# A two-layer hybrid block on one core: three feature groups by sevens in three gate-and-up blocks of each feed-forward layer, with other buffers for the weight loads

## The chip, the cores and the metric

The kernel runs on one core of one Trainium2 chip. The metric is the time of one execution on the device in microseconds (us). The kernel before takes 2230.15 us, the median of 3 runs (2229.86 to 2231.21).

The engines are named as in the profile. PE is TensorE, the matrix engine; PEld is its loading of the stationary operand, which runs beside the matmuls. DVE is VectorE, ACT is ScalarE, POOL is GpSimd, and SP is SyncE, which here only issues DMAs. All five run their own instruction streams in order and wait for each other at semaphores.

## What is computed

The input is 256 tokens of 2048 features in float32. There are two layers. The first has a gated delta rule beside a gated linear recurrence, the second two kinds of attention. Each is followed by a feed-forward part, which is the part that the change touches:

```python
def rmsnorm(x, w):
    xf = x.astype(jnp.float32)
    y = xf * lax.rsqrt(jnp.mean(xf * xf, axis=-1, keepdims=True) + NORM_EPS)
    return (y * w.astype(jnp.float32)).astype(x.dtype)

def swiglu(hn, w_gate, w_up, w_down):
    return (jax.nn.silu(hn @ w_gate) * (hn @ w_up)) @ w_down

def reference(x, ...):
    h = x
    for layer in range(DEPTH):
        ...
        h = h + swiglu(rmsnorm(h, ffn_norm[layer]), ffn_w_gate[layer], ffn_w_up[layer], ffn_w_down[layer])
    return rmsnorm(h, final_norm)
```

The gate and the up matrix are 2048 by 5632 each, the down matrix is 5632 by 2048, all float32 and read from HBM once.

## The kernel before

**Products in three matmuls.** A float32 weight tile of 128 by 1024 arrives by DMA (512 KB). ACT copies it into a type of fewer bits (`whi` or `thi`, line 608), DVE subtracts that from the original and keeps the rest (`wlo` or `tlo`, line 620). The activations `X` are kept as such a pair too. `Mix.add` then adds high by high (line 473), high by low (line 474) and low by high (line 475). So a weight tile costs an ACT cast, a DVE subtraction and some matmuls of 512 columns, and the second matmul of a tile is the first to need the low half.

**The feed-forward part** (`ffn`, line 720) works in three stages. A stage has four (the last one three) blocks of gate and up columns, 512 of each, and then two down blocks, which add the stage's inner values `hid` into the residual `h`. Within a block the contraction runs over feature groups of 512 features, of which a gate-and-up block has four. A group is done in one of two ways.

- *Plain* (`simple`): four weight tiles, each multiplied with both halves of the tokens, 12 matmuls a tile, 48 in all.
- *By sevens* (`seven`, line 490): a 2 by 2 block product with seven products in place of eight, 6 matmuls each, 42 in all. It needs sums of weight tiles and of activation tiles. Four tiles are loaded by SP: `ha` (called b11 in the code), `hb` (b12), `hc` (b22) and one that uses the tag `raw` (b21). DVE adds b12 into b11 (`first_sum`, line 503) and later b22 into it (`second_sum`, line 508). POOL issues two DMAs of 512 KB that add from HBM into a tile that is there already: b22 into b12 (line 504) and, later, b21 into b11 (line 512). The sums of activation tiles (`comb`) are made once per group by `combine_x` (line 404), on DVE with one cast on ACT, or by `combine` from a block's inner values.

A table (line 790) says how many groups of each block go by sevens. `(0, 2, 2, 2), (2, 2)` is the first stage: four gate-and-up blocks with none, two, two and two groups, then two down blocks with two each. I count the blocks of a layer from 0: 0 to 3 and 4, 5 are the first stage; 6 to 9 and 10, 11 the second; 12 to 14 and 15, 16 the third.

**Order.** `ffn` lists all steps of a layer in one order (lines 810 to 823), a step being one weight tile or sum and its matmuls. A block's steps by sevens are split: the first four products of every group (`early`) go between the last four plain steps of the block ahead (`tail`), the other three (`direct`) are mixed two to one with the block's own remaining plain steps (`body`). From block 1 on DVE, ACT and PE run just in the order in which `stream` (line 566) emits, with high halves made four steps ahead of the matmuls and low halves three. There are six buffers for high halves and five for low halves, so the low half of a step can be written only when PE has done the step five before it.

Other work hangs on this order by `puts`: when a block is done, `gate` and `product` make its inner values, `first` (line 729) transposes them on PE into `Ph` and copies them by ACT, `second` (line 746) makes their low half on DVE, and for the first blocks of a stage `combine` follows in parts on DVE (lines 396 and 401).

**Load buffers.** A step's tag names its buffers. `raw` has five, three of them in the pool `wr`, which is there for the whole kernel, and two in the phase's own pool `mx`; `ha`, `hb` and `hc` have two each in `mx`. Memory of a phase pool was used by the phase before, so its first user waits until that phase is over. In the first block of a layer, which is all plain, the tags `raw`, `ha`, `raw`, `hb`, `raw`, `hc` are taken in turn (line 487), to start with many buffers. `loads_to` (line 577) issues loads up to eight steps ahead, in the order of the steps. A tile's buffer comes free when the low half that is last to read it is done; for b11 that is the seventh product's.

Of the kernel before, what the change touches and what calls it, by code (L numbers as in the profile page):

```python
# [4 lines left out]
F32, F32R, I32 = dt.float32, dt.float32r, dt.int32  # L5
# [42 lines left out]
def body(tc, A, out):  # L48
    nc = tc.nc
# [7 lines left out]
    wr = pool("wr", 3)  # L57
# [4 lines left out]
    mx, ogp, fp = Phase(), Phase(), Phase()  # L62
# [18 lines left out]
    h = res.tile([128, 2, D], F32, name="h")  # L81
    X = res.tile([128, NK, 2, T], F32R, name="X", tag="X")
# [321 lines left out]
    def combine_x(x4, r=None):  # L404

        f = mx.tile([128, 4, T], F32, name="cf", **(dict(tag="de", bufs=1) if more else dict(tag="T", bufs=2)))
        V.tensor_tensor(out=f, in0=x4[:, :, 0].bitcast(F32), in1=x4[:, :, 1].bitcast(F32), op=ALU.add)
        return run(combine([f[:, :, t * 128:(t + 1) * 128] for t in range(2)], r))
# [36 lines left out]
    class Mix:  # L445
# [34 lines left out]
        def simple(self, i, u, first):  # L480
            b = {}

            def use(w, tt=(0, 1)):
                for t in tt:
                    self.add(t, i, lambda kk: self.xs(2 * u + kk, t), w)
            k = 2 * u + i
            return Step(("raw", "ha", "raw", "hb", "raw", "hc")[k % 6] if first and k < 10 else "raw",
                        lambda raw: nc.sync.dma_start(raw, self.src(i, u)), use, unit=(i, use))

        def seven(self, m):  # L490
# [75 lines left out]
    def stream(order, puts, guard):  # L566

        at = [0, 0, 0]
        where = {id(y): k for k, y in enumerate(order)}
        g = None

        slots, count_raw = {}, [0]

        def loads_to(n, must=False):
            while at[2] < min(n, len(order)):
                y = order[at[2]]
                if y.tag:  # L580
                    q = slots.setdefault(y.tag, [])
                    if len(q) == (5 if y.tag == "raw" else 2):
                        k = where[id(q[0])]
                        if k >= at[1]:
                            if not must:
                                return
                            low(k)
                        q.pop(0)
                    q.append(y.free)
                    if y.tag == "raw":  # L590
                        count_raw[0] += 1
                    y.raw = (wr.tile([128, 1024], F32, name="raw") if y.tag == "raw" and count_raw[0] % 5 in (0, 2, 4) else
                             mx.tile([128, 1024], F32, name=y.tag, tag=y.tag, bufs=2))
                    y.load(y.raw)
                at[2] += 1

        def ahead(n):

            while at[0] < min(n + 1, len(order)):
                y, k = order[at[0]], at[0]  # L600
                loads_to(k + 1, True)
                for z in y.needs:
                    low(where[id(z)])
                if y.ready:
                    y.raw = y.ready()
                y.hi = (fp.tile([128, 1024], F32R, name="thi", tag="thi", bufs=2) if k % 6 in (1, 4) else
                        wh.tile([128, 1024], F32R, name="whi"))
                S.copy(y.hi, y.raw)  # L608
                at[0] += 1
                if at[0] > 1:  # L610
                    low(at[0] - 2)
            while at[1] < min(n, len(order)):
                low(at[1])

        def low(k):
            while at[1] <= k:
                y, j = order[at[1]], at[1]
                y.lo = (fp.tile([128, 1024], F32R, name="tlo", tag="tlo", bufs=2) if j % 5 in (1, 3) else
                        wl.tile([128, 1024], F32R, name="wlo"))
                V.tensor_sub(y.lo, y.raw, y.hi.bitcast(F32))  # L620
                at[1] += 1
                if y.after:
                    y.after()

        for n, y in enumerate(order):
            for f in puts.get(n, []):
                f()
            if y is guard:
                g = tc.manual_schedule(engines={V.engine, S.engine, PE.engine})
                g.__enter__()  # L630
            loads_to(n + 8)
            ahead(n + 1 + 3)
            y.use((y.hi, y.lo))
            if y.unit:
                tick()
        for n in sorted(k for k in puts if k >= len(order)):
            for f in puts[n]:
                f()
        if g is not None:
            g.__exit__(None, None, None)  # L640
# [79 lines left out]
    def ffn(L, then, fin=None):  # L720

        gu, dn = A[f"gu{L}"], A[f"dn{L}"]
        cx, ch, blocks = {}, {}, []
# [64 lines left out]

        hid = ogp.tile([128, 16, 2, T], F32R, name="hid", tag="hid")
        b, events = 0, []  # L790
        for groups, down in (((0, 2, 2, 2), (2, 2)), ((2, 2, 2, 2), (2, 2)), ((2, 2, 2), (1, 1))):
            piece = len(groups)
            for j in range(piece + 2):
                space = (msp, "ms") if len(blocks) % 2 else (acc, "acc")
                if j < piece:
                    Y = Mix(lambda i, u, b=b: gu[b, u, i], lambda k: X[:, k], {m: lambda m=m: cx[m] for m in range(groups[j])}, 4,
                            *space, first=b == 0)
                    Y.after = values(Y, hid, j, j < max(down))
                    b += 1
                else:  # L800
                    p = j - piece
                    Y = Mix(lambda i, u, u0=2 * (b - piece), p=p: dn[2 * p + i, u0 + u], lambda k: hid[:, k],
                            {m: lambda m=m: ch[m] for m in range(down[p])}, piece, *space)
                    Y.after = residual(Y, p)
                blocks.append(Y)
# [5 lines left out]
        for Y in blocks:  # L811
            e = list(Y.early)
            r = -(-len(e) // len(tail)) if tail else 0
            while e or tail:
                order += e[:r] + tail[:1]
                e, tail = e[r:], tail[1:]
            cut = len(Y.plain) - 4 * (Y is not blocks[-1])
            d, body, tail = list(Y.direct), Y.plain[:cut], Y.plain[cut:]
            Y.first = (d + body + tail)[0]
            while d or body:  # L820
                order += d[:2] + body[:1]
                d, body = d[2:], body[1:]
            events += (Y.middle() if Y.ns else []) + Y.after
        where = {id(y): k for k, y in enumerate(order)}
# [4 lines left out]
        p0 = [where[id(y)] for y in blocks[0].plain]  # L829
        put(p0[5], lambda: cx.update({0: combine_x(X[:, 0:4])}))  # L830
        put(p0[8], rstd)
        put(p0[10], lambda: cx.update({1: combine_x(X[:, 4:8])}))
        Z, Y = blocks[-2:]
        q = where[id(Y.first)]
        if fin:
# [767 lines left out]
```

## Time and profile before

| | us |
|---|---|
| median of 3 runs | 2230.15 |
| the profiled execution, its time | 2229.7 |
| the profiled execution, its span from first to last instruction | 2227.5 |
| first layer's mixer, feed-forward part | 0 to 432, 432 to 1110 |
| second layer's mixer, feed-forward part and end | 1110 to 1524, 1524 to 2227 |

The limits of the stages are read from the chain of work that ended last. The page of the profile gives each engine's busy time, a strip of 40 slices, the DMA queues, that chain, and the costliest groups of instructions. In a row of instructions, `L620 DVE TENSOR_TENSOR wlo<-ha,whi` is line 620 on DVE, which writes `wlo` from `ha` and `whi`; in the timeline the first two columns are start and duration in us, `xN` merges N instructions in a row, and brackets at the end hold the idle time before it and who ended it. The duration of a pipelined instruction reaches beyond the start of the next one, so the distance of starts is what one costs in a full queue. In a list of waits the three numbers are the us in total, how often, and the longest.

### The profile page before, as it was taken

The numbers are of one execution on the slowest core, as the hardware profiler recorded it, in microseconds if no ns is written. First come the engines' busy times: TensorE is split into PE (matmuls) and PEld (weight loads), VectorE is DVE, ScalarE is ACT, GpSimd is POOL, SyncE is SP. The second block draws the span as 40 slices with busy tenths as digits, with TensorE's granted clock in tenths as the row PEclk, the third lists the DMA queues.
The fourth block names the chain that finished last, engine by engine and source line by source line (L and its number), as shares of the span: only waits on it lengthen the run. The fifth ranks groups of instructions, "written<-read, shape, count | busy, mean of one in ns | idle before, by whom it ended". The sixth has DMA issues, their size and how long they took to land.

```text
span 2227.5 us, 30574 instructions
## 1 busy us (share of the span) xinstructions
PE 2203.5 (99%) x10960; PEld 1844.0 (83%) x10960; DVE 1829.3 (82%) x2554; ACT 1341.4 (60%) x1775; POOL 106.2 (5%) x126
## 2 busy tenths in 40 slices
PE   9999999999999999999999999999999999999998
PEld 8888888788888888888888888887888888888886
DVE  8899676679888888888786688857888888988886
ACT  6776664556665666666654554445665566665665
POOL 0000000000100000000000000000000100100000
PEclk9999999999999999999999999999999999999999
DMA  7445446687988888888555455566788887888884
GB/s 285 156 146 166 139 149 187 206 256 228 257 267 247 237 284 237 264 255 253 171 188 158 156 186 171 162 184 221 219 255 277 237 274 245 238 272 249 234 263 133
DMA packets 135209, 485.25 MB, mean 218 GB/s; under 512 B 15088, under 2 KB 16624, under 8 KB 134928
## 3 DMA queue, kind: packets, MB, share of 16 engines
q1 hardware_dynamic: 117488, 420.10, 54.6%
q0 software_dynamic: 17280, 62.92, 16.4%
q8 instruction: 86, 1.41, 0.3%
q14 instruction: 67, 0.55, 0.1%
q10 hardware_dynamic: 288, 0.27, 0.0%
HBM read 481.13 MB, written 2.10 MB: 217 GB/s over the span
## 4 chain that ended last, share of the span: by engine, by line
PE 97%; DVE 1%; DMA 1%; ACT 0%; issue 0%; DVEq 0%; ACTq 0%; SPq 0%
PE F L474 20%; PE F L473 20%; PE F L475 20%; PE Pw L201 11%; PE Pw L206 6%; PE Px L305 3%; PE Px L306 3%; PE Px L307 3%; PE F L420 1%; PE F L421 1%; PE Ph L735 1%; PE F L419 1%; PE Psc L1365 1%; PE Pw L247 0%; PE Pt L328 0%; PE Pw L248 0%
## 5 line engine op out<-in xcount | busy, mean ns | idle before, releaser
L181 ACT CAST whi<-raw 128x1024 fp32r<-128x1024 f32 x245 | 256.8, 1051 | 266.3 <-PE Pw L201 86.4
L182 DVE TENSOR_TENSOR wlo<-raw,whi 128x1024 fp32r<-128x1024 f32 x245 | 298.8, 1220 | 118.7 <-PE Px L306 37.7
L201 PE MATMUL Pw<-X,whi 128*128 128x512 f32 x1088 | 388.4, 400 | 0.0
L608 ACT CAST whi<-raw 128x1024 fp32r<-128x1024 f32 x238 | 249.4, 1054 | 109.9 <-PE F L475 88.1
L206 PE MATMUL Pw<-X,wlo 128*128 128x256 f32 x1088 | 304.8, 280 | 0.1
L473 PE MATMUL F<-whi,X 128*128 128x512 f32 x712 | 279.2, 393 | 9.9 <-ACT whi L608 9.9
L475 PE MATMUL F<-whi,X 128*128 128x512 f32 x712 | 278.2, 391 | 0.0
L608 ACT CAST whi<-ha 128x1024 fp32r<-128x1024 f32 x152 | 160.5, 1056 | 167.0 <-DVE ha L503 41.4
L201 PEld LDWEIGHTS Pw<-X,whi 128*128 128x128 f32 x1088 | 204.2, 188 | 47.2 <-issue 0.5
L474 PE MATMUL F<-wlo,X 128*128 128x512 f32 x588 | 230.4, 392 | 0.1
L206 PEld LDWEIGHTS Pw<-X,wlo 128*128 128x128 f32 x1088 | 205.4, 189 | 1.5 <-DVE wlo L182 0.7
L620 DVE TENSOR_TENSOR wlo<-raw,whi 128x1024 fp32r<-128x1024 f32 x140 | 170.3, 1219 | 4.6 <-ACT whi L608 0.9
L473 PEld LDWEIGHTS F<-whi,X 128*128 128x128 f32 x712 | 134.4, 189 | 37.9 <-ACT whi L608 10.4
L474 PE MATMUL F<-tlo,X 128*128 128x512 f32 x420 | 163.4, 389 | 0.0
L475 PEld LDWEIGHTS F<-whi,X 128*128 128x128 f32 x712 | 134.4, 189 | 27.9
L620 DVE TENSOR_TENSOR wlo<-ha,whi 128x1024 fp32r<-128x1024 f32 x96 | 117.4, 1222 | 37.4 <-ACT whi L608 25.6
L608 ACT CAST thi<-ha 128x1024 fp32r<-128x1024 f32 x92 | 97.3, 1057 | 76.4 <-DVE ha L503 32.6
L474 PEld LDWEIGHTS F<-wlo,X 128*128 128x128 f32 x588 | 111.2, 189 | 24.4 <-DVE wlo L620 1.5
L473 PE MATMUL F<-whi,hid 128*128 128x512 f32 x336 | 131.2, 390 | 0.0
L475 PE MATMUL F<-whi,hid 128*128 128x512 f32 x336 | 130.8, 389 | 0.0
L608 ACT CAST thi<-raw 128x1024 fp32r<-128x1024 f32 x100 | 105.2, 1052 | 36.7 <-PE F L475 32.1
L474 PE MATMUL F<-wlo,hid 128*128 128x512 f32 x320 | 124.5, 389 | 0.0
(444 smaller groups left out, 4887.8 us busy)
## 6 DMA issues: line engine op xcount, KB each, us to landing
raw<-in_gu SPq DMA_DIRECT2D x222, 512.0 KB, 5.5
raw<-in_dn SPq DMA_DIRECT2D x116, 512.0 KB, 4.9
raw<-in_w0w SPq DMA_DIRECT2D x72, 512.0 KB, 3.7
raw<-in_wo SPq DMA_DIRECT2D x64, 512.0 KB, 3.7
raw<-in_w1w SPq DMA_DIRECT2D x64, 512.0 KB, 3.7
ha<-in_gu SPq DMA_DIRECT2D x44, 512.0 KB, 5.2
hb<-in_gu SPq DMA_DIRECT2D x44, 512.0 KB, 7.6
hc<-in_gu SPq DMA_DIRECT2D x42, 512.0 KB, 5.6
```

Of the source, the lines that this page charges most:

```text
L181: S.copy(hi, raw)
L182: V.tensor_sub(lo, raw, hi.bitcast(F32))
L201: PE.matmul(P.rearrange("p a b -> p (a b)"), hi[:, kk], X[:, k].rearrange("p a b -> p (a b)"), start=k == 0, stop=False)
L206: PE.matmul(P[:, 0], lo[:, kk], X[:, k, 0], start=False, stop=k == NK - 1)
L305: PE.matmul(Ps[t], x[:, 0, ts], hi[:, kk], start=k == 0, stop=False)
L306: PE.matmul(Ps[t], x[:, 0, ts], lo[:, kk], start=False, stop=False)
L307: PE.matmul(Ps[t], x[:, 1, ts], hi[:, kk], start=False, stop=k == n - 1)
L473: PE.matmul(P, xh, hi[:, kk], start=z[0] == 1 and kk == 0, stop=False, skip_group_check=skip)
L474: PE.matmul(P, xh, lo[:, kk], start=False, stop=False, skip_group_check=skip)
L475: PE.matmul(P, xl, hi[:, kk], start=False, stop=kk == 1 and z[0] in z[1:], skip_group_check=skip)
L608: S.copy(y.hi, y.raw)
L620: V.tensor_sub(y.lo, y.raw, y.hi.bitcast(F32))
```

## The change

The table gets a 3 in the second block of each stage: blocks 1, 7 and 13 do three feature groups by sevens and one plainly. For the third group the sums of X are needed. They have no buffer of their own: `third` makes them in the part of `hid` that belongs to the fourth inner block, which is not yet written, or read for the last time, when block 1, 7 or 13 needs them. It is called once a stage: ahead of plain step 12 of block 0, and two steps after the first direct step of blocks 6 and 12. A block with three groups by sevens has only four plain steps; it leaves three of them (in place of four) to the `tail`.

The load buffers are shared out anew. `ha`, `hb` and `hc` get three buffers each, `raw` keeps the three of the pool `wr` and loses the two in `mx`, and the first block takes the `raw` buffers alone. The scratch for POOL's DMA descriptors is halved.

```diff
-            k = 2 * u + i
-            return Step(("raw", "ha", "raw", "hb", "raw", "hc")[k % 6] if first and k < 10 else "raw",
+            return Step("first" if first else "raw",
                         lambda raw: nc.sync.dma_start(raw, self.src(i, u)), use, unit=(i, use))
...
-        slots, count_raw = {}, [0]
+        slots = {}
+        bufs = dict(wr=3, ha=3, hb=3, hc=3)
...
                 if y.tag:
-                    q = slots.setdefault(y.tag, [])
-                    if len(q) == (5 if y.tag == "raw" else 2):
+                    tag = y.tag if y.tag in bufs else "wr"
+                    q = slots.setdefault(tag, [])
+                    if len(q) == bufs[tag]:
...
-                    y.raw = (wr.tile([128, 1024], F32, name="raw") if y.tag == "raw" and count_raw[0] % 5 in (0, 2, 4) else
-                             mx.tile([128, 1024], F32, name=y.tag, tag=y.tag, bufs=2))
+                    y.raw = (wr.tile([128, 1024], F32, name="raw") if tag == "wr" else
+                             mx.tile([128, 1024], F32, name=tag, tag=tag, bufs=bufs[tag]))
...
-        for groups, down in (((0, 2, 2, 2), (2, 2)), ((2, 2, 2, 2), (2, 2)), ((2, 2, 2), (1, 1))):
+        for groups, down in (((0, 3, 2, 2), (2, 2)), ((2, 3, 2, 2), (2, 2)), ((2, 3, 2), (1, 1))):
...
-            cut = len(Y.plain) - 4 * (Y is not blocks[-1])
+            cut = len(Y.plain) - (4 if Y.ns < 3 else 3) * (Y is not blocks[-1])
...
+        def third():
+            r = hid[:, 12:16].rearrange("p k a t -> p (k a t)").rearrange("p (h i k n) -> p h i k n", h=2, i=4, k=2)
+            cx[2] = combine_x(X[:, 8:12], r)
+        put(p0[12], third)
+        for Y in (blocks[6], blocks[12]):
+            put(where[id(Y.first)] + 2, third)
...
-    nc = _bacc.Bacc("TRN2", target_bir_lowering=False, num_devices=1, dynamic_dma_scratch_size=8192)
+    nc = _bacc.Bacc("TRN2", target_bir_lowering=False, num_devices=1, dynamic_dma_scratch_size=4096)
```

In the changed kernel the lines of `Step` calls and of `stream` stand one lower (a load of a plain step is L487 in place of L488, a subtraction L619 in place of L620).

Two places show how the instruction streams move. The first is the queue of SP at the passage from the first mixer to the first feed-forward part; the names in brackets are the semaphores waited for, and a wait for PE and Activation together is the one for the old phase's memory. Before:

```order
L488 DMA raw<-in_gu 128x1024 [waits DMAHW1_49,DVE_49,Activation_49]
L488 DMA raw<-in_gu 128x1024 [waits DMAHW2_49,DVE_49]
L488 DMA raw<-in_gu 128x1024 [waits DMAHW3_49,DVE_49]
L488 DMA raw<-in_gu 128x1024 [waits PE_49,Activation_49]
L488 DMA ha<-in_gu 128x1024
L488 DMA hb<-in_gu 128x1024
L488 DMA raw<-in_gu 128x1024
L488 DMA hc<-in_gu 128x1024
```

Of the change:

```order
L487 DMA raw<-in_gu 128x1024 [waits DMAHW1_49,DVE_49,Activation_49]
L487 DMA raw<-in_gu 128x1024 [waits DMAHW2_49,DVE_49]
L487 DMA raw<-in_gu 128x1024 [waits DMAHW3_49,DVE_49]
L487 DMA raw<-in_gu 128x1024 [waits DMAHW4_49,DVE_49]
L487 DMA raw<-in_gu 128x1024 [waits DMAHW6_49,DVE_49]
L498 DMA ha<-in_gu 128x1024 [waits PE_49,Activation_49]
L498 DMA ha<-in_gu 128x1024 x2
L487 DMA raw<-in_gu 128x1024 [waits DMAHW5_49,DVE_49]
```

Before, the three loads ahead of the wait for the old phase are of the third, seventh and ninth step, and the first step's own load is the one that waits. In the change five loads stand ahead of that wait, the first step's among them.

The second place is DVE's stream in block 1 of the first layer before, and its counterpart, from the low halves of the inner values of the block ahead (L748, L747) on. `ha` after the arrow is a b11. Before, in the passage from block 1 to block 2, whose transposes are those of block 0:

```order
L748 TENSOR_TENSOR hid<-Ph,hid 128x4x128 x2
L396 TENSOR_TENSOR cc_5155<-f 128x256 x2
L620 TENSOR_TENSOR tlo<-ha,thi 128x1024
L620 TENSOR_TENSOR wlo<-raw,whi 128x1024
L396 TENSOR_TENSOR cc_5155<-cc_5155,f 128x256
L620 TENSOR_TENSOR tlo<-raw,whi 128x1024
L620 TENSOR_TENSOR wlo<-ha,thi 128x1024
L396 TENSOR_TENSOR cc_5155<-f,cc_5155 128x256
L620 TENSOR_TENSOR wlo<-ha,whi 128x1024
L401 TENSOR_TENSOR comb<-cc_5155,comb 128x1024
L503 TENSOR_TENSOR ha<-ha,hb 128x1024
L620 TENSOR_TENSOR tlo<-raw,whi 128x1024
```

Of the change:

```order
L747 TENSOR_TENSOR hid<-Ph,hid 128x4x128 x2
L396 TENSOR_TENSOR cc_5210<-f 128x256 x2
L619 TENSOR_TENSOR wlo<-ha,whi 128x1024
L619 TENSOR_TENSOR tlo<-ha,whi 128x1024
L396 TENSOR_TENSOR cc_5210<-cc_5210,f 128x256
L619 TENSOR_TENSOR wlo<-ha,thi 128x1024
L619 TENSOR_TENSOR tlo<-ha,whi 128x1024
L396 TENSOR_TENSOR cc_5210<-f,cc_5210 128x256
L502 TENSOR_TENSOR ha<-ha,hb 128x1024
L619 TENSOR_TENSOR wlo<-ha,whi 128x1024
L401 TENSOR_TENSOR comb<-cc_5210,comb 128x1024
L619 TENSOR_TENSOR wlo<-ha,thi 128x1024
```

Before, one seventh product (the first `tlo<-ha`), two plain steps and then block 2's first products of its two groups follow. In the change the three seventh products of block 1 follow, and behind them at once block 2's first products and sums, with no plain step between.

More of the change, by code (lines that the diff above doesn't have):

```diff
@@ L589, in loads_to @@
                     q.append(y.free)
-                    if y.tag == "raw":
-                        count_raw[0] += 1
-                    y.raw = (wr.tile([128, 1024], F32, name="raw") if y.tag == "raw" and count_raw[0] % 5 in (0, 2, 4) else
-                             mx.tile([128, 1024], F32, name=y.tag, tag=y.tag, bufs=2))
+                    y.raw = (wr.tile([128, 1024], F32, name="raw") if tag == "wr" else
+                             mx.tile([128, 1024], F32, name=tag, tag=tag, bufs=bufs[tag]))
                     y.load(y.raw)
```

## The prediction

> **What bounds the kernel now.** I read the page's busy times first, then its chain of work that ended last, then PE's own waits, then the windows of one block.
>
> ```profile
> PE 2203.5 (99%) x10960; PEld 1844.0 (83%) x10960; DVE 1829.3 (82%) x2554; ACT 1341.4 (60%) x1775; POOL 106.2 (5%) x126
> PE 97%; DVE 1%; DMA 1%; ACT 0%; issue 0%; DVEq 0%; ACTq 0%; SPq 0%
> PE F L473 <- ACT whi L608: 9.9, 2, 5.0
> core 0: us, PE busy (x) PEld busy (x) DVE busy (x) ACT busy (x) POOL busy (x), PEclk, DMA share, GB/s
> 540.90:582.60 41.70, 41.70 (x190) 34.63 (x189) 37.54 (x39) 27.36 (x31) 3.46 (x4) 1.00 0.82 253
> ```
>
> PE is the bound, and it waits in the feed-forward parts only twice, about 5 us each. But in a block with two groups by sevens (540.9 to 582.6) DVE is busy 37.5 of 41.7 us: it is the second limit, 4 us behind. The change takes work from PE and gives it to DVE.
>
> **What a matmul costs.** The transposes of two such blocks in a row:
>
> ```profile
> 499.19 0.87 PE Ph L735 x8
> 540.88 0.87 PE Ph L735 x8
> ```
>
> A block has 14 products by sevens of 6 matmuls and 8 plain tiles of 12, 180 matmuls; 41.69 less 0.87 us, over 180, is 0.2268 us each. (The 391 ns of the groups overlap.) So a product by sevens is 1.36 us, a plain tile 2.72 us. Six groups a kernel go from 48 to 42 matmuls: 36 fewer, **8.2 us off PE**.
>
> **The start of a feed-forward part.** The rows of the first one:
>
> ```profile
> 430.92 0.42 PEld L328 LDWEIGHTS Pt<-tab,h 128*128 128x128 f32 x4 [0.53 <-DVE h L361]
> 431.60 0.42 PEld L328 LDWEIGHTS Pt<-tab,h 128*128 128x128 f32 x4 [0.26 <-DVE h L361]
> 420.25 2.96 SPq L488 DMA_DIRECT2D raw<-in_gu  x2
> 432.39 0.33 SPq L488 DMA_DIRECT2D raw<-in_gu  x1
> 436.03 1.99 ACT L608 CAST whi<-raw 128x1024 fp32r<-128x1024 f32 x2 [2.21 <-DMA raw<-in_gu]
> 437.12 1.22 PE L473 MATMUL F<-whi,X 128*128 128x512 f32 x2 [4.87 <-ACT whi L608]
> 441.22 0.39 PE L473 MATMUL F<-whi,X 128*128 128x512 f32 x1
> 437.00:439.00 2.00, 1.83 (x4) 1.03 (x5) 1.90 (x2) 2.00 (x4) 0.00 (x0) 0.50 0.99 408
> ```
>
> The first step's load goes out at 432.39, when the old phase's memory is free, and PE idles 4.87 us for it. Then the granted clock is 0.50: nine matmuls start in the 4.10 us from 437.12 to 441.22, where 2.04 us would do, so 2.06 us more are lost. In the change the first three loads take the place of those issued up to 423.2, and their casts stand in ACT's queue ahead of the last squares and transposes of the mixer. PE goes from the transposes straight on. **Off: 9.9 in both parts for the wait, and 4.1 for the slow clock, 14.0 us.** Next late would be the second step, whose cast still needs phase memory; but PE has some 20 matmuls (4.5 us) of the first and third step before it. With three `raw` buffers a buffer's turn is a load (3.6 us from 432.39 to 436.03), a cast and a subtraction (1.05 and 1.22), about 6 us against 8.2 us of PE for three plain steps: hidden.
>
> **DVE in the passage from three groups to two.** This decides. Here is the same place in block 2 before (relative to the transposes, its rows stand for block 1, 7 and 13):
>
> ```profile
> 540.72 1.03 PE L735 MATMUL Ph<-tab,a 128*128 128x128 f32 x8
> 541.51 0.48 PE L473 MATMUL F<-thi,X 128*128 128x512 f32 x1
> 542.95 1.29 DVE L748 TENSOR_TENSOR hid<-Ph,hid 128x512 fp32r<-128x512 f32 x2 [3.06 <-ACT f L744]
> 544.16 0.75 DVE L396 TENSOR_TENSOR cc<-f 128x256 f32<-128x256 f32 x2
> 544.83 1.22 DVE L620 TENSOR_TENSOR tlo<-ha,whi 128x1024 fp32r<-128x1024 f32 x1
> 545.96 1.22 DVE L620 TENSOR_TENSOR wlo<-raw,whi 128x1024 fp32r<-128x1024 f32 x1
> 547.10 0.42 DVE L396 TENSOR_TENSOR cc<-cc,f 128x256 f32<-128x256 f32 x1
> 547.43 1.22 DVE L620 TENSOR_TENSOR wlo<-raw,thi 128x1024 fp32r<-128x1024 f32 x1
> 549.66 1.05 ACT L608 CAST whi<-ha 128x1024 fp32r<-128x1024 f32 x1 [2.46 <-DMA ha<-in_gu]
> 550.74 1.23 DVE L620 TENSOR_TENSOR wlo<-ha,whi 128x1024 fp32r<-128x1024 f32 x1 [0.62 <-ACT whi L608]
> 551.88 1.22 DVE L401 TENSOR_TENSOR comb<-cc,comb 128x1024 fp32r<-128x1024 f32 x1
> ```
>
> DVE stands still until PE has transposed and ACT has copied; this wait resets its lead over PE whatever lead it had. From the starts, a full-size DVE operation costs 1.135 us and a quarter 0.33. With t = 0 at the transposes (540.72): the first low half behind them is done at 5.33 (544.83 + 1.22), and PE's next step begins at 0.79, so that after four steps it wants that low half. Before, the four steps are two sevens, a plain one and a seven, 6.80 us; the low half is wanted at 0.79 + 6.80 + 0.23 = 7.8, a lead of 2.5 us. In the change all four are sevens, 5.44 us: wanted at 6.5, lead 1.1.
>
> Two things then come at once. First, the next block's b11 needs a buffer that this very step frees. Before, a b11 buffer freed at 546.05 was loaded and in ACT's hands at 549.66, 3.6 us later, with four steps (8.2 us of PE) in between; in the change it is three sevens, 4.1 us. Second, seven products and four sums in a row cost DVE 1.135 us each, with PE at 1.36 us a product. Step by step, low half done against wanted:
>
> - three seventh products: done 5.3, 6.5, 7.9; wanted 6.5, 7.9, 9.2. No wait.
> - block 2's first product: b11 in hand at 5.33 + 3.6 = 8.95, cast 1.05, subtraction 1.22: 11.25; wanted 10.6. **0.65.**
> - the next: a quarter operation, the first sum, its low half: 13.85; wanted 12.6. **1.25.**
> - the next: `comb` (L401) and its low half: 16.1; wanted 15.2. **0.9.**
> - the plain step: sum and low half: 18.4; wanted 17.5. **0.9.**
> - then 20.7 against 21.1, 22.95 against 22.45 (**0.5**), 24.1 against 24.3; from there on no sums, and PE's 2.72 us of the next plain step restore the lead.
>
> That is **4.2 us a passage**; three a layer (blocks 1 to 2, 7 to 8, 13 to 14), six in all: 25.2 us. Were the load no matter, DVE alone would give what remains without its 2.2 us of standing still, 2.0 a passage.
>
> **The third combination.** DVE's queue gets `third` in one piece, with a wait for ACT in its middle: 1.14 + 4 × about 0.36 + a cast of 1.05 with two hand-overs (0.2) + 1.14 = 5.0 us, six times; what queues behind it are the low halves.
>
> ```profile
> 702.97 1.22 DVE L620 TENSOR_TENSOR tlo<-raw,whi 128x1024 fp32r<-128x1024 f32 x1
> 747.40 1.03 PE L735 MATMUL Ph<-tab,a 128*128 128x128 f32 x8
> L399 ACT CAST comb<-cc 128x1024 fp32r<-128x1024 f32 x7 | 7.3, 1045 | 0.4 <-DVE cc L396 0.4
> ```
>
> In block 6 it comes behind the low half that is done at 704.19. PE's step for it begins 174 matmuls ahead of 747.40, at 707.9; its lead is 4.0 us. Add PE's 1.36, take off 5.0 and a low half: minus 0.75. So 0.75 us of wait in block 6 and in block 12. In block 1 the lead at that place is the four steps that five low buffers allow less a low half and a sum's debt, 4.7 us; behind it come three sums, and the same account goes to minus 0.9 and once more to minus 0.5: 1.4 us. Per layer 2.9, **in all 5.8 us**; bounds 0 (ACT's part hidden and the lead a microsecond better) and 10.
>
> **Other parts at nothing.** ACT's three more casts a group lie in its idle third. The extra POOL additions land long before their products: eight steps (13.6 us) lie between a sum and its b12 product where six (10.9) did. Blocks with two groups pass to one another with a buffer more than before. I take the halved descriptor scratch at nothing, since only six additions of 512 KB are in a block; it can't gain, and would cost at most the wait of an addition (7.4 us landing) where it is full.
>
> **Sum.** 2229.7 − 8.2 − 14.0 + 25.2 + 5.8 = 2238.5 for the profiled execution. PE can put a few of the first step's matmuls into the 0.8 us (0.53 and 0.26) that it waits ahead of the last transposes: four matmuls, −0.9 in both parts. The median lies 0.45 above the profiled execution: **2238 us**, 0.35% slower. What a measurement can tell from no change is about 0.2%, 4.5 us.
>
> **Rivals.**
> - *The loads don't matter.* b11 arrives in time (buffers freed sooner than I count, or waits elsewhere that give DVE its lead back); DVE alone makes 2.0 a passage: 13 us less, 2225, and down to 2207 with no waits at all. For it: `raw` loads stop early in a block of three groups, so the DMA engines may be idle then. Against: the row of 549.66 shows ACT waiting 2.46 us for just this load, when it had four steps' time. This is the case in which the kernel becomes faster; it decides where the wait for `ha` no longer shows on ACT.
> - *The loads are later.* The page has
>
> ```profile
> q1 hardware_dynamic: 117488, 420.10, 54.6%
> q0 software_dynamic: 17280, 62.92, 16.4%
> ha<-in_gu SPq DMA_DIRECT2D x44, 512.0 KB, 5.2
> ```
>
>   801 loads' worth of 512 KB in 54.6% of 2227.5 us is 1.52 us each of all 16 DMA engines, 120 additions in 16.4% 3.04 each. A block of three groups has 16 loads and six additions, 42.6 us, against 40.3 us of PE. Its loads could then take the median 5.2 in place of 3.6 us: 6 × 1.6, 2248. Against: the place is followed by sums that need no load.
> - *The clock.* The window of 437 to 439 shows the clock at 0.50 after a wait of 4.87 us. If PE's waits in a passage (4.2 of some 15 us, none over 1.25) drop it too, each passage costs the 2.06 us of the start again: 6 × 2.06, 2250. For it: no row shows the clock after several short waits. Against: it was 1.00 from 540.9 to 582.6, and PE does two thirds of its work in a passage. [...]
> - *The start saves nothing*, because the second step waits for phase memory as long as the first did: 14.0 us more, 2252. The order of the matmuls (those of the third step ahead of the second's) speaks against it.
>
> **How the numbers follow.** Forecast 0.5 (2231 to 2245; mostly slower, a quarter within 0.2%), loads that don't matter 0.25 (2207 to 2231), later loads 0.17, clock or start 0.08. The range leaves out the case without any waits and the far end of the last two: 2220 to 2250. Faster 0.24, same 0.18, slower 0.58.
>
> **What would show it.** Right: PE's first L473 in both feed-forward parts without a 5 us wait and at clock 1.00; PE waits for `wlo` L619 in five or six steps behind the transposes in blocks 2, 8 and 14, four us a passage, with ACT waiting for `ha` there; smaller ones behind L401 `hid`. Wrong: no waits of PE's on L619, or such waits in other blocks, where a load in the three `raw` buffers is late.

## The result, and the profile after

| | before | after |
|---|---|---|
| time, median | 2230.6 us (2229.9 to 2231.2) | 2258.0 us (2256.7 to 2263.7) |
| profiled execution, its span | 2229.7, 2227.5 | 2257.4, 2255.2 |
| PE waits on L473 and L474 in the feed-forward parts | 10 us | 32.0 us |

The ratio of the means is 1.0128, with a 95% interval of 1.011 to 1.0146. The medians lie 27.4 us apart, where 7.9 were forecast, and 2258.0 us lies outside the forecast range of 2220 to 2250. Two lines of the page after, the busy times and the chain of work that ended last:

```profile
PE 2209.9 (98%) x10924; PEld 1830.9 (81%) x10924; DVE 1880.2 (83%) x2620; ACT 1353.4 (60%) x1799; POOL 116.4 (5%) x138
PE 85%; DVE 7%; DMA 4%; issue 3%; ACT 1%; DVEq 0%; ACTq 0%; SPq 0%
```

The 36 matmuls are gone (10,960 to 10,924), but the chain, which was 97% PE before, is 85% PE now and runs through DVE (7%) and DMA (4%) as well. PE's waits in the feed-forward parts (us in total, times, longest; lines of the changed kernel stand one lower than before's, so L619 makes the low half and L607 the high half):

```profile
PE F L474 <- DVE wlo L619: 17.6, 25, 1.2
PE F L474 <- DVE tlo L619: 10.7, 21, 0.8
PE F L473 <- ACT whi L607: 3.7, 8, 0.8
```

54 waits, none over 1.2 us. The two 5 us waits at the start have gone; this is the first step there now, and the clock behind it (the column after POOL):

```profile
429.97 0.39 PE L307 MATMUL Px<-whi,Od 128*128 128x512 f32 x1
430.19 0.39 PE L473 MATMUL F<-whi,X 128*128 128x512 f32 x1
```

```profile
433.00:437.00 4.00, 4.00 (x19) 3.20 (x18) 4.00 (x8) 2.18 (x3) 0.00 (x0) 1.00 0.82 257
```

PE goes from the mixer's last products straight on, at a granted clock of 1.00. The passage from block 13 to 14 shows the mechanism that was forecast, almost step by step: ACT's wait for b11, then PE's waits.

```profile
1021.84 1.05 ACT L607 CAST whi<-ha 128x1024 fp32r<-128x1024 f32 x1 [3.49 <-DMA ha<-in_gu]
1022.94 0.49 PE L473 MATMUL F<-whi,X 128*128 128x512 f32 x1 [0.31 <-ACT whi L607]
1024.20 0.50 PE L474 MATMUL F<-tlo,X 128*128 128x512 f32 x1 [0.77 <-DVE tlo L619]
1026.81 0.50 PE L474 MATMUL F<-wlo,X 128*128 128x512 f32 x1 [0.95 <-DVE wlo L619]
1029.07 0.50 PE L474 MATMUL F<-wlo,comb 128*128 128x512 f32 x1 [0.61 <-DVE wlo L619]
1031.35 0.51 PE L474 MATMUL F<-tlo,X 128*128 128x512 f32 x1 [0.61 <-DVE tlo L619]
1036.01 0.50 PE L474 MATMUL F<-tlo,comb 128*128 128x512 f32 x1 [0.29 <-DVE tlo L619]
```

These are 3.5 us of idle time (forecast: 4.2). What was not forecast lies ahead of it. ACT's three longest rows of waits for gate and up weights that SP loads, after, and then the only row of before for `raw` loads of these weights:

```profile
ACT whi L607 <- DMA raw<-in_gu: 54.8, 35, 4.0
ACT whi L607 <- DMA ha<-in_gu: 34.9, 19, 3.7
ACT thi L607 <- DMA raw<-in_gu: 31.5, 19, 3.5
```

```profile
ACT whi L608 <- DMA raw<-in_gu: 4.6, 2, 2.4
```

ACT waits 86 us for `raw` loads of gate and up weights, 4.6 before (for `ha` it waited 27 us before already). The end of block 1 shows why: first SP's queue in the timeline, then the DMA engines in the windows (last two columns: busy share, GB/s), then the load groups between 486 and 512 us (how many, KB each, median us to landing):

```profile
489.26 0.33 SPq L498 DMA_DIRECT2D raw<-in_gu  x1
492.66 0.33 SPq L498 DMA_DIRECT2D raw<-in_gu  x1
497.45 7.45 SPq L487 DMA_DIRECT2D raw<-in_gu  x3
507.88 2.93 SPq L498 DMA_DIRECT2D ha<-in_gu  x3
```

```profile
490.00:494.00 4.00, 4.00 (x19) 3.33 (x18) 4.00 (x6) 3.97 (x5) 0.00 (x0) 1.00 1.02 373
```

```profile
raw<-in_gu SPq DMA_DIRECT2D x5, 512.0 KB, 8.5
```

Then the casts and the low half on which PE waits there, and PE:

```profile
499.68 1.05 ACT L607 CAST whi<-raw 128x1024 fp32r<-128x1024 f32 x1 [4.57 <-PE Ph L734]
502.23 1.05 ACT L607 CAST thi<-raw 128x1024 fp32r<-128x1024 f32 x1 [1.50 <-PE F L474]
503.32 1.23 DVE L619 TENSOR_TENSOR wlo<-raw,thi 128x1024 fp32r<-128x1024 f32 x1 [1.33 <-ACT thi L607]
```

```profile
504.60 0.50 PE L474 MATMUL F<-wlo,X 128*128 128x512 f32 x1 [0.62 <-DVE wlo L619]
507.91 0.50 PE L474 MATMUL F<-wlo,X 128*128 128x512 f32 x1 [1.18 <-DVE wlo L619]
```

The DMA engines are full (busy share 1.01 to 1.03 from 490 to 502), and the five `raw` loads take 8.5 us in the median, in place of the 3.6 of the forecast. Each goes out only when a buffer comes free. The two late ones are b21 tiles (L498), issued at 489.26 and 492.66, right behind low halves of earlier `raw` tiles that end at 489.23 and 492.64. Taken singly, they need 10.3 and 9.5 us, so they land at 499.6 and 502.2, where ACT's casts begin. The profile puts these two waits down to PE. But with a fourth `raw` buffer (below) the first of the two casts runs ahead of the transposes, so it doesn't depend on them; and at the same place of blocks 7 and 13 the profile names the `raw` load for both.

The three b21 products of the block stand in a row on PE, at 1.36 us each. The low half of the third is done at 504.55, and PE waits for it at 504.60. Then PE waits at 507.91 for the first seventh product. The forecast had no wait at either step.

### The profile page after: what moved, and what is told of

The parts are those of the page before. It is cut to its first block, busy times and chain, and to the rows that moved or that the text cites. A ratio compares the mean times of both kernels' runs of the same rounds, so it can differ in the third digit from the quotient of the medians.

```text
span 2255.2 us, 30546 instructions
## 1 busy us (share of the span) xinstructions
PE 2209.9 (98%) x10924; PEld 1830.9 (81%) x10924; DVE 1880.2 (83%) x2620; ACT 1353.4 (60%) x1799; POOL 116.4 (5%) x138
## 4 chain that ended last, share of the span: by engine, by line
PE 85%; DVE 7%; DMA 4%; issue 3%; ACT 1%; DVEq 0%; ACTq 0%; SPq 0%
PE F L474 17%; PE F L475 16%; PE F L473 16%; PE Pw L201 11%; PE Pw L206 6%; PE Px L305 3%; PE Px L307 3%; PE Px L306 3%; DVE wlo L619 3%; DMA raw<-in_gu 2%; DVE tlo L619 1%; DMA ha<-in_gu 1%; PE F L420 1%; PE F L421 1%; PE F L419 1%
## 5 line engine op out<-in xcount | busy, mean ns | idle before, releaser
L181 ACT CAST whi<-raw 128x1024 fp32r<-128x1024 f32 x245 | 256.8, 1050 | 266.4 <-PE Pw L201 84.0
L182 DVE TENSOR_TENSOR wlo<-raw,whi 128x1024 fp32r<-128x1024 f32 x245 | 298.8, 1220 | 119.8 <-PE Px L306 37.9
L607 ACT CAST whi<-raw 128x1024 fp32r<-128x1024 f32 x220 | 231.0, 1052 | 156.2 <-DMA raw<-in_gu 54.8
L607 ACT CAST whi<-ha 128x1024 fp32r<-128x1024 f32 x182 | 190.5, 1054 | 162.5 <-DVE ha L502 56.3
L473 PE MATMUL F<-whi,X 128*128 128x512 f32 x640 | 251.6, 393 | 3.7 <-ACT whi L607 3.7
L475 PE MATMUL F<-whi,X 128*128 128x512 f32 x640 | 250.2, 391 | 0.0
L474 PE MATMUL F<-wlo,X 128*128 128x512 f32 x580 | 228.6, 394 | 14.5 <-DVE wlo L619 14.5
L619 DVE TENSOR_TENSOR wlo<-raw,whi 128x1024 fp32r<-128x1024 f32 x124 | 151.2, 1220 | 32.7 <-ACT whi L607 27.1
L607 ACT CAST thi<-raw 128x1024 fp32r<-128x1024 f32 x110 | 115.4, 1052 | 71.3 <-DMA raw<-in_gu 31.5
L474 PE MATMUL F<-tlo,X 128*128 128x512 f32 x368 | 145.3, 395 | 8.2 <-DVE tlo L619 8.2
L619 DVE TENSOR_TENSOR wlo<-ha,whi 128x1024 fp32r<-128x1024 f32 x116 | 141.4, 1219 | 14.1 <-PE F L474 8.6
L473 PEld LDWEIGHTS F<-whi,X 128*128 128x128 f32 x640 | 120.4, 188 | 33.1 <-ACT whi L607 8.3
L474 PEld LDWEIGHTS F<-wlo,X 128*128 128x128 f32 x580 | 109.1, 188 | 45.1 <-DVE wlo L619 23.0
L619 DVE TENSOR_TENSOR tlo<-raw,whi 128x1024 fp32r<-128x1024 f32 x96 | 117.0, 1218 | 30.6 <-ACT whi L607 29.9
L473 PE MATMUL F<-whi,hid 128*128 128x512 f32 x360 | 140.5, 390 | 0.0
L475 PE MATMUL F<-whi,hid 128*128 128x512 f32 x360 | 140.2, 389 | 0.0
L475 PEld LDWEIGHTS F<-whi,X 128*128 128x128 f32 x640 | 120.5, 188 | 23.9
L607 ACT CAST thi<-ha 128x1024 fp32r<-128x1024 f32 x82 | 86.4, 1054 | 72.3 <-DVE ha L502 24.8
```

The costliest lines, as they stand in the source:

```text
L181: S.copy(hi, raw)
L182: V.tensor_sub(lo, raw, hi.bitcast(F32))
L473: PE.matmul(P, xh, hi[:, kk], start=z[0] == 1 and kk == 0, stop=False, skip_group_check=skip)
L474: PE.matmul(P, xh, lo[:, kk], start=False, stop=False, skip_group_check=skip)
L475: PE.matmul(P, xl, hi[:, kk], start=False, stop=kk == 1 and z[0] in z[1:], skip_group_check=skip)
```

## Experiments

Each was timed beside the kernel before on one chip; the chips differ, but the kernel before reads 2230.8 to 2231.3 us on all of them, so the times can be compared to about half a us. First the parts of the change by themselves.

**The first loads alone**, in the kernel before with its buffers:

```diff
-  ("raw", "ha", "raw", "hb", "raw", "hc")[k % 6] if first and k < 10 else "raw"
+  ("raw", "raw", "raw", "ha", "hb", "hc")[k % 6] if first and k < 10 else "raw"
-  ... wr.tile(...) if y.tag == "raw" and count_raw[0] % 5 in (0, 2, 4)
+  ... wr.tile(...) if y.tag == "raw" and count_raw[0] % 5 in (1, 2, 3)
```

> The kernel before, with one thing changed: the first three loads of a feed-forward part go into the three old `wr` buffers; two groups by sevens everywhere, five `raw` buffers. The theory (the start is worth 14.0 us, as predicted: 9.9 of waits and 4.1 of slow clock): 2216 us. Rival (the second step waits as the first did, and the after kernel's quiet start hides the same loss later): 2226 to 2231.

Measured: 2214.9 us, ratio 0.9928 (0.9913 to 0.9943). The start is worth 15.9 us; 14.9 were forecast.

**The new buffers with two groups:** the kernel after with a table of twos, without `third`.

```diff
-  ((0, 3, 2, 2), (2, 2)), ((2, 3, 2, 2), (2, 2)), ((2, 3, 2), (1, 1))
+  ((0, 2, 2, 2), (2, 2)), ((2, 2, 2, 2), (2, 2)), ((2, 2, 2), (1, 1))
-  put(p0[12], third)
-  for Y in (blocks[6], blocks[12]): put(where[id(Y.first)] + 2, third)
```

> The kernel after, with two groups by sevens in place of three and no third combination: the new buffers (three for `raw`, three each for ha, hb, hc), the first loads and the halved scratch alone. As the prediction had it (three `raw` buffers cost nothing): the time of the kernel with the first loads alone, 2216 us, within 3. The theory now (ACT waits for `raw` loads some 130 us in the kernel after where it waited 5, so three `raw` buffers are late): 2220 to 2232, with PE waits for L619 outside the passages. Rival (they are late beside three groups only): 2216.

Measured: 2213.9 us, the same as with the first loads alone. The rival holds: beside two groups three `raw` buffers and the halved scratch cost nothing, taken together with the third `ha`, `hb` and `hc` buffers, although ACT waits 92 us for `raw` loads:

```profile
ACT whi L607 <- DMA raw<-in_gu: 59.6, 41, 4.0
ACT thi L607 <- DMA raw<-in_gu: 32.5, 18, 4.2
```

So ACT's waiting by itself is no cost here: PE doesn't wait at L473, L474 or L475 in this kernel.

**`third` alone:** the same with its three calls put back.

> The kernel after, with two groups by sevens in place of three, but the third combination still made (nothing reads it): its price alone, against the kernel with the buffers alone. By the prediction 5.8 us, or somewhat less since block 1 has one sum fewer behind it: 4 to 6. By the gaps of PE in the trace of after (0.9 in blocks 6 and 12 each, 1.6 in block 1): 6 to 7. Rival (ACT's part and the lead hide it): 0 to 2.

Measured: 2222.9, so 9.0 us, above each of the ranges given. PE's waits in this kernel are 5.7 us in nine times, nearly the forecast 5.8:

```profile
PE F L474 <- DVE wlo L619: 4.0, 6, 1.1
PE F L474 <- DVE tlo L619: 1.7, 3, 0.7
```

What is missing is the price of a wait beyond its idle time. Three rows of the kernel after:

```profile
1626.26 0.39 PE L473 MATMUL F<-whi,X 128*128 128x512 f32 x1
1627.24 0.50 PE L474 MATMUL F<-tlo,X 128*128 128x512 f32 x1 [0.60 <-DVE tlo L619]
1627.58 0.39 PE L475 MATMUL F<-whi,X 128*128 128x512 f32 x1
```

From 1626.26 to 1627.58 are 1.32 us, where two matmuls in the flow take 0.45. Of the 0.87 more only 0.60 is marked as idle: the matmul ahead is waited out to its end and the one behind runs 0.50, in all 0.27 us. The nine waits of this kernel, read in the same way, give 0.27 or 0.28 us each, and 45 of the 54 in the kernel after give 0.28 in the median (0.27 to 0.40; the other nine stand at slow clock or right before another wait). Nine such waits are 2.4 us, which makes 8.1 of the 9.0.

**One buffer more**, as a fourth `raw` (the diff) and, in a second kernel, as a fourth `ha` (ha=4, wr=3); the memory comes from the descriptor scratch.

```diff
-  wr = pool("wr", 3)
-  bufs = dict(wr=3, ha=3, hb=3, hc=3)
+  wr = pool("wr", 4)
+  bufs = dict(wr=4, ha=3, hb=3, hc=3)
-  dynamic_dma_scratch_size=4096
+  dynamic_dma_scratch_size=1024
```

> The kernel after with a fourth `raw` buffer (its memory from a descriptor scratch of 1024 bytes in place of 4096). If the waits in the passages came from the buffers of b11 and from DVE, as predicted, only what lies outside them goes: some 10 us of waits at the end of block 1's direct products and in blocks 2, 8 and 14, so 2246 to 2253. If three `raw` buffers are what made the passages longer too (ACT waits for `raw` ahead of the transposes, so DVE enters with no lead): 2236 to 2246. If `raw` is no matter: 2258; more than 2258 if the small scratch makes the additions wait.

> The kernel after with a fourth `ha` buffer in place of a fourth `raw` one (memory from the small scratch again). If b11's late buffer is the first cause of a passage, as predicted (4.2 us with it, 2.0 without): six passages by 2.2 us less, some 13 us, and the wait of ACT for `ha` goes: 2243 to 2248. If DVE's own work is what holds PE, and the late load only stands beside it: 2252 to 2258, with the same PE waits for L619.

Measured: 2242.7 and 2242.5, each 15 us less than after. The first lies in the range given for late `raw` loads that lengthen the passages too, the second 0.5 us below its range. With a fourth `raw` buffer each b21 load goes out one buffer sooner (the third at 489.45 in place of 492.66), the last `raw` loads of block 1 are issued in half the time, and b11 follows 3.6 us sooner (the two kernels stand within 0.2 us of each other at 484):

```profile
497.64 3.64 SPq L487 DMA_DIRECT2D raw<-in_gu  x3
504.29 2.94 SPq L498 DMA_DIRECT2D ha<-in_gu  x3
```

With a fourth `ha` buffer the first waits of a passage go and four of 2.0 us stay, the forecast's "DVE alone":

```profile
766.36 0.50 PE L474 MATMUL F<-wlo,X 128*128 128x512 f32 x1 [0.48 <-DVE wlo L619]
768.63 0.51 PE L474 MATMUL F<-wlo,comb 128*128 128x512 f32 x1 [0.61 <-DVE wlo L619]
770.90 0.50 PE L474 MATMUL F<-tlo,X 128*128 128x512 f32 x1 [0.63 <-DVE tlo L619]
775.57 0.50 PE L474 MATMUL F<-tlo,comb 128*128 128x512 f32 x1 [0.29 <-DVE tlo L619]
```

Both kernels have a smaller scratch too, and two gains of the same size could be one. So a second set keeps the scratch at 4096 and takes the memory from a `comb` buffer:

```diff
-  ((0, 3, 2, 2), (2, 2)), ((2, 3, 2, 2), (2, 2)), ((2, 3, 2), (1, 1))
+  ((0, 3, 2, 2), (1, 1)), ((2, 3, 2, 2), (1, 1)), ((2, 3, 2), (1, 1))
-  r = fp.tile([128, 2, 4, 2, 128], F32R, name="comb", tag="comb", bufs=4)
+  r = fp.tile([128, 2, 4, 2, 128], F32R, name="comb", tag="comb", bufs=3)
```

> The kernel after, with one group by sevens in every down block in place of two in the first two stages; this needs three `comb` buffers in place of four, so 8 KB are free for the next three kernels. Eight groups of 48 matmuls in place of 42: 48 x 0.2268 = 10.9 us more than after, 2265 to 2270; the base for the next three.

> The same with a fourth `raw` buffer, and the descriptor scratch as in after. If the buffer gave the 15 us of the kernel with four `raw` buffers: 15 less than the base. If the smaller scratch gave them: as the base.

> The base with a fourth `ha` buffer, three `raw`, scratch as in after. By the buffer 15 us less than the base, by the scratch nothing.

> The base with four `raw` and four `ha` buffers. If late `raw` loads and the late b11 are two causes, each with 15 us of its own: 25 to 30 less than the base. If it is one wait that either buffer relieves (loads go out in one order, so a late one holds the next): 15 to 19 less.

Measured: 2266.2, 2253.4 (`raw`), 2251.7 (`ha`), 2237.8 (both): 12.8, 14.4 and 28.3 us less. It is the buffers, not the scratch, and they add: late `raw` loads and the late b11 are two causes. In this second set the mean granted clock of each profiled run is 0.999; in the first set it is 0.998 in the kernel after, which has one stretch at 0.50 (last section), and 0.999 in the kernel with four `ha` buffers, so by estimate some 1.6 of its 15.5 us may be the clock. With both cured a passage keeps 1.4 to 2.3 us of idle time, 9.8 us in 20 waits over all six:

```profile
1020.19 0.50 PE L474 MATMUL F<-tlo,comb 128*128 128x512 f32 x1 [0.48 <-DVE tlo L619]
1022.46 0.50 PE L474 MATMUL F<-wlo,X 128*128 128x512 f32 x1 [0.62 <-DVE wlo L619]
1027.13 0.50 PE L474 MATMUL F<-tlo,comb 128*128 128x512 f32 x1 [0.29 <-DVE tlo L619]
```

Then DVE's part of a passage, in steps on top of the fourth `raw` buffer (2242.7). **`third` in five pieces** in blocks 6 and 12: parts(k) puts the first sum, three steps of combine and its rest at the steps k to k + 4.

```diff
-  for Y in (blocks[6], blocks[12]): put(where[id(Y.first)] + 2, third)
+  for Y in (blocks[6], blocks[12]): parts(where[id(Y.first)] + 2)
```

> Four `raw` buffers, and `third` in blocks 6 and 12 cut into five pieces at five steps in a row, in place of one piece (block 1's stays whole). If the single piece is what PE waits for there: the four waits of 0.74 us go, with what each costs beyond its idle time (0.27 by the rows of after: 0.50 in place of 0.39 for the first matmul, 0.16 of drain), so 4 us less than the kernel with four `raw` buffers: 2238 to 2240. If it is DVE's total work in these blocks: no change, 2242 to 2243.

Measured: 2238.3, 4.4 us less; the four waits are gone. It was the single piece.

**Three groups in the last block of a stage** (3, 9, 14), `third` in pieces in the block before:

```diff
-  ((0, 3, 2, 2), (2, 2)), ((2, 3, 2, 2), (2, 2)), ((2, 3, 2), (1, 1))
+  ((0, 2, 2, 3), (2, 2)), ((2, 2, 2, 3), (2, 2)), ((2, 2, 3), (1, 1))
```

> Four `raw` buffers, and the three groups in the last gate and up block of a stage (blocks 3, 9, 14), with `third` in five pieces in the block before. The passage then leads into a down block, behind which no combination of inner values is made: per passage 2.5 us less of DVE (two L396 operations of 0.33, three quarters and `comb`'s 1.14). If DVE's work in the passage decides: 2 us or less of waits a passage, 2215 to 2226. If the three seventh products and b11's buffer decide, whatever follows: passages as before, 4 us of waits or more, 2232 to 2240.

Measured: 2241.9, above both ranges, and 3.6 us more than with `third` in pieces and three groups in the old place. The first theory is refuted: without any combination in the passage PE waits about as much, now for the down block's b11 too. The mean granted clock of its profiled run is 0.997, where it is 0.999 with `third` in pieces and three groups in the old place.

```profile
594.24 0.50 PE L473 MATMUL F<-thi,hid 128*128 128x512 f32 x1 [0.86 <-ACT thi L607]
595.50 0.50 PE L474 MATMUL F<-wlo,hid 128*128 128x512 f32 x1 [0.76 <-DVE wlo L619]
597.89 0.50 PE L474 MATMUL F<-tlo,hid 128*128 128x512 f32 x1 [0.72 <-DVE tlo L619]
601.44 0.50 PE L474 MATMUL F<-wlo,X 128*128 128x512 f32 x1 [0.50 <-DVE wlo L619]
```

**Standing still, and short steps.** Three edits on the kernel with `third` in pieces (2238.3): the subtraction for `hid` two steps later; two plain steps in place of one among a three-group block's direct products; both.

```diff
-  [(3, first), (4, second)] + ([(6, part), (8, part), (9, last)] if want else [])
+  [(3, first), (6, second)] + ([(8, part), (10, part), (11, last)] if want else [])
-  cut = len(Y.plain) - (4 if Y.ns < 3 else 3) * (Y is not blocks[-1])
+  cut = len(Y.plain) - (4 if Y.ns < 3 else 2) * (Y is not blocks[-1])
```

> As the kernel with four `raw` buffers and `third` in pieces (2238.3), but the subtraction for `hid` (L747) and the combination of inner values come two steps later behind the transposes. If DVE loses its lead by standing still for them, as predicted (2.2 us of a passage): the waits for L619 behind it shrink by about 2 us a passage, 2226 to 2231. If the five low buffers set the lead anyway: 2236 to 2240. If the combination now falls among the sums of the next block: waits there, 2238 to 2245.

> As the kernel with four `raw` buffers and `third` in pieces (2238.3), but a block of three groups puts two of its four plain steps among its own direct products and leaves two for the next block's early products (one and three before). If PE's short steps (1.36 us) behind the transposes are what DVE can't follow: a plain step there gives it 1.6 us, and b11's buffer is no earlier; 2228 to 2234. If the density of sums in the next block's early products decides (one plain step fewer among them): 2238 to 2248.

> Both: the subtraction for `hid` two steps later, and two plain steps of a block of three groups among its direct products. If the two causes add (each some 1.6 to 2 us a passage): 2217 to 2226. If they are one and the same lead, counted twice: as the better of the two alone.

Measured: 2239.2, 2235.4 and 2234.7. The first edit alone does nothing. The second lies between its two ranges, and both together are hardly better than the second alone. The rows of DVE and ACT at that place say why:

```profile
755.35 1.23 DVE L619 TENSOR_TENSOR wlo<-ha,whi 128x1024 fp32r<-128x1024 f32 x1 [4.49 <-ACT whi L607]
```

```profile
752.32 1.07 ACT L737 CAST hid<-Ph 128x512 fp32r<-128x512 f32 x2 [2.83 <-PE Ph L734]
```

DVE no longer waits at L747, but at the next low half, whose cast stands in ACT's queue behind ACT's own wait for the transposes. The second edit leaves 3.0 us of idle time in the passage from block 7 to 8, as before it (0.53, 0.95, 0.61, 0.61 and 0.30), but in three waits in place of five:

```profile
767.43 0.50 PE L474 MATMUL F<-wlo,X 128*128 128x512 f32 x1 [1.70 <-DVE wlo L619]
769.82 0.50 PE L474 MATMUL F<-tlo,comb 128*128 128x512 f32 x1 [0.74 <-DVE tlo L619]
773.37 0.50 PE L474 MATMUL F<-tlo,X 128*128 128x512 f32 x1 [0.54 <-DVE tlo L619]
```

The whole kernel has 24 waits in place of 35; eleven at 0.27 are 3.0 us, and 2.9 were gained. So ACT's copies of `Ph` for `hid` and `f`, which were in `first`, were moved too (as `copies`), with either placing of the plain steps:

```diff
-  [(3, first), (4, second)] + ...
+  [(3, first), (6, copies), (7, second)] + ([(9, part), (11, part), (12, last)] if want else [])
```

> As the kernel with four `raw` buffers and `third` in pieces (2238.3), but ACT's copies of the transposed block (L737 and L743 of after), and with them all that follows, come three steps later behind the transposes. With the subtraction alone moved, DVE's standing still only changed its line: it waited 4.49 us for a cast of `ha` that stood behind ACT's own wait for the transposes (2.83). If this standing still is what costs DVE its lead, now on both engines: a passage loses 2 us or more of its waits, 2220 to 2231. If DVE's sums among the short steps decide, whatever the lead: 2234 to 2240.

> The same with two plain steps of a block of three groups among its direct products (2235.4 with the copies where they were). If lead and short steps are both causes: 2214 to 2225, and with no wait left it would come to 2210. If only the density of sums counts: 2232 to 2237.

Measured: 2231.2 and 2225.6, so 7.1 and 9.7 us less than with the copies early. Both are causes: standing still on ACT and DVE together, and the short steps. They came out at and just above the upper ends of their ranges; in the second kernel one wait of 1.6 to 1.9 us a passage is left, for a low half behind `comb` (L401) and a second sum (L507), and one more of 0.7 us in the first passage of each layer.

**All cures, in the last block of a stage:**

> Three groups in the last gate and up block of a stage, four `raw` buffers, `third` in five pieces in the block before, ACT's copies of the transposed block three steps later, two plain steps of the block of three among its direct products. What is left in the kernel with the same edits but three groups in the old place (2225.6) is one wait of 1.6 to 1.9 us a passage behind `comb` and the second sums, and some 2 us a part at `third` in block 1. If the combination of inner values, which this place doesn't have, makes that wait now that the lead is kept: 2211 to 2219, about the two-group kernel with the new start (2214), and this is the only version of three groups that could beat it. If the way into a block of three (three first sums among short steps; 1.2 us of waits each with the three groups in the last block before) or the loads of the down block come in its place: 2220 to 2232.

Measured: 2231.3, in the second range. Waits of 0.2 to 0.8 us stand on the way into the block and behind it, and two longer ones for ACT's copy of a middle sum (L539, 1.87 and 1.81 us). No version with three groups came under the two-group kernels with the new start (2214).

## Why the prediction was wrong

The sum of the forecast beside what the runs give (us):

| step | forecast | measured | from |
|---|---|---|---|
| 36 matmuls fewer | −8.2 | not alone | count of the page |
| start of both parts | −14.9 | −15.9 | first loads alone |
| three `raw` buffers | 0 | 12.8 to 15.3 | fourth `raw`, two sets |
| passages: b11's buffer | 13.2 | 14.4 to 15.5 | fourth `ha`, two sets |
| passages: DVE alone | 12.0 | 12 to 15 | what is left of 27.4; 15 by the waits with both buffers |
| `third` | 5.8 | 9.0 | `third` alone |

- **Fewer matmuls:** 36 went, as counted; the price of 8.2 is the forecast's own, and the last but one row leans on it. The nearest test is the base of the second set: 48 matmuls more took 8.2 us more, where this price gives 10.9 and the stretch of slow clock in the kernel after (mean clock 0.998, 0.999 in the base) may hide 1.6.
- **The start: right.** No 5 us wait, clock 1.00, and 15.9 us. (The prediction's sum took off 0.9 us once for the matmuls ahead of the last transposes; four of them in each part, as it says, would be 1.8.)
- **The `raw` buffers: the step that failed.** The prediction put a buffer's turn at "a load (3.6 us from 432.39 to 436.03), a cast and a subtraction (1.05 and 1.22), about 6 us against 8.2 us of PE for three plain steps: hidden". Beside two groups no wait showed. Beside three, where the waits begin, the load takes 8.5 us in the median, which makes the turn 10.8, more than the 8.2. Nor are the steps plain there: the three b21 products in a row are 4.1 us of PE. Late loads in the three `raw` buffers were the prediction's own last sign of being wrong. The 3.6 us came from a moment when loads had just begun (DMA busy share 0.00 from 428 to 432); the trace of before has a median of 5.5 us for these loads over the whole program, in its issue groups,

```profile
raw<-in_gu SPq DMA_DIRECT2D x222, 512.0 KB, 5.5
```

That median would still have made the turn only 7.8 us: it is the loaded stretch that counts. And the prediction's own account of a three-group block, 42.6 us of DMA against 40.3 of PE, was used for b11 alone and not for `raw`. Some 14 of the 19.5 us of the miss are here.
- **The passage: right in mechanism and nearly in size.** b11 and DVE were to cost 25.2 us and cost 26 to 30. That DVE stands still is right too, but the prediction saw it on DVE's wait alone: ACT stands in front of the same transposes (2.83 us with the subtraction moved), so moving DVE's operation by itself gains nothing.
- **`third`: right in idle time, low in price.** 5.7 us of idle time against 5.8; every wait costs 0.27 more, a term that the forecast lacks. The whole kernel after has 54 waits: 32.0 us idle and 14.6 beside. With a stretch of slow clock (below) that is some 48 of the 51.5 us that lie between 2258.0 and 2230.6 − 15.9 − 8.2; 3 us stay unassigned. The same sum leaves 0.7 to 2.8 us open in the eight other kernels with three groups in the second block and two in each down block, with 12 to 40 waits, so most of that isn't tied to the waits.
- **The other parts at nothing:** the halved scratch showed no cost beside two groups, and a smaller one still took nothing off what the fourth buffers gained; beside three groups the halving was not tried by itself. ACT's casts and POOL's additions were not tried by themselves.
- **The rivals.** Loads that don't matter: refuted by the fourth `ha`. Later loads: near in time (2248), but the late ones are `raw`, while the first b11 of the passages out of blocks 1 and 13 is in ACT's hands 3.7 us after its load goes out, as forecast (3.6). The start that saves nothing: refuted. The clock: it fell to 0.50 in one passage of six, by estimate for about 1.6 us in all.

## What to carry to other kernels

A buffer's turn is worked out with the load time of the stretch it serves, where its own DMA demand is highest (here 8.5 us in the median, against the 3.6 of the forecast and a median of 5.5 over the whole program), and with the steps that take the buffer there, not with the fastest load of the trace and the longest steps. An engine's waits are counted as well as added up, since here each took some 0.27 us of PE beside its idle time. Where a wait on one engine is to be moved, look whether the engine that feeds it stands before the same event, as ACT did here before the transposes (2.83 us). Here only the first loads pay: with two groups they make 2214 us, 0.72% under the kernel before (0.57 to 0.87%).

## What the runs showed of the hardware

TensorE's granted clock fell from 1.00 to 0.50 after a row of short waits. In the first passage of the second feed-forward part (PEclk is the third column from the end):

```profile
1617.20:1620.60 3.40, 1.87 (x7) 1.02 (x6) 1.78 (x3) 2.15 (x3) 0.00 (x0) 1.00 0.70 280
1621.00:1623.00 2.00, 1.83 (x5) 0.95 (x4) 2.00 (x3) 1.86 (x3) 0.86 (x1) 0.50 0.00 0
```

No wait there was over 1.2 us, and PE was busy 1.87 of 3.40 us, yet the clock went to 0.50 for about 3.5 us, where matmuls start every 0.42 us in place of 0.23; eight of them cost some 1.6 us, an estimate from these distances. The other five passages, with nearly the same waits, kept 1.00. With a fourth `raw` buffer the clock fell once too: PE was busy 1.04 of the 3.00 us from 509 to 512, and the clock was 0.50 from 513.2 to 515.9. With later copies and two plain steps PE was busy 1.73 of the 3.50 us from 1606 to 1609.5, and the clock was 0.50 from 1611 to 1613.4. With all cures in the last block matmuls start every 0.42 to 0.43 us from 1069.55 to 1072.53, behind a wait of 1.87 us. What decides between a passage that keeps its clock and one that loses it, no run here shows.
